# Two Strassen pairs instead of one in three gate/up stages, with the low parts of ten weight chunks made by adding DMA transfers

## The chip, the core and the metric

The kernel runs on one core of a Trainium2 chip: TensorE (PE in the profile) multiplies, VectorE (DVE) and ScalarE (ACT) work on tiles, GpSimd (POOL) does small odd jobs, and SyncE (SP) issues the DMA transfers, which 16 DMA engines carry out. The metric is the device time of one execution in microseconds (us); lower is better.

## The reference

The program is a two-layer transformer trunk on 256 rows of 1024 numbers, in fp32. Each layer is a half-weighted SwiGLU feed-forward block, an attention block, and a second feed-forward block:

```
def rmsnorm(x, g):
    x32 = x.astype(jnp.float32)
    y = x32 * lax.rsqrt(jnp.mean(x32 * x32, axis=-1, keepdims=True) + EPS)
    return (y * g.astype(jnp.float32)).astype(x.dtype)

def swiglu(h, w_gate, w_up, w_down):
    return (jax.nn.silu(h @ w_gate) * (h @ w_up)) @ w_down

    for i in range(DEPTH):
        h = rmsnorm(x, ffn1_norm[i])
        x = x + 0.5 * swiglu(h, ffn1_w_gate[i], ffn1_w_up[i], ffn1_w_down[i])
...
        x = x + jnp.concatenate([o_s, o_m], axis=-1) @ w_out[i]

        h = rmsnorm(x, ffn2_norm[i])
        x = x + 0.5 * swiglu(h, ffn2_w_gate[i], ffn2_w_up[i], ffn2_w_down[i])
```

`w_gate` and `w_up` are 1024 x 2816, `w_down` is 2816 x 1024. There are four feed-forward blocks; the code names them (layer, number): (0, 1), (0, 2), (1, 1), (1, 2). The change touches the gate/up stage (the products with `w_gate` and `w_up`) of the last three.

## The kernel before

**Three products for one.** Every fp32 operand is split in two: a high part `hi`, the value rounded to the type fp32r that TensorE takes, and a low part `lo = value - hi`. A product of two blocks is then three matmuls (`dense`, L498 to L519): hi by hi (L508), lo by hi (L511) and hi by the activations' low part (L514).

**Chunks.** A gate/up stage has 11 groups of 256 columns (`g` = 0 to 10), and each group has two chunks (`c` = 0, 1), halves of the 1024 rows. A chunk, written g/c below, is 512 rows by 256 gate and 256 up columns, 1 MB, laid out as 128 partitions x 2048. It goes through these steps:

- `loader` (L284) issues two 512 KB transfers on SP into a tile `raw`. There are three such tiles (`NRAW`), and a load goes out only when one of them is free.
- `split_hi` (L315) makes `hi` on ScalarE (L335), for a plain chunk in two casts of 128 x 1024. There are four pairs of hi and lo tiles (`NHL`); a chunk's first cast waits until TensorE has used up the chunk four places before it.
- `split_lo` (L339) makes `lo` on VectorE (L353), for a plain chunk in two subtractions of 128 x 1024. When the last is done, the `raw` tile is free.
- TensorE runs 24 matmuls for the chunk: two row blocks of 128, four pieces of 128 rows, three passes (`plain_chunk`, L740).

When both chunks of a group are done, `evac` (L614) applies silu and the product on ScalarE and VectorE, and turns the result by way of DRAM (`hd`, `hr`) for the down products that follow.

**A pair.** `PAIR` (L375) names one pair of groups in each of the last three stages, groups 3 and 4. Its four chunks are taken together as the blocks 11, 12, 22, 21 of a 2 x 2 block product and multiplied by a scheme of Strassen's kind: seven products `m1` to `m7` of 12 matmuls (`product`, L813) instead of eight. Three products use a block as it is (`b11`, `b22`, `b21`), four use a sum of blocks (`t1` to `t4`, `sums` in `pair_items`, L398). A sum takes four VectorE subtractions of 128 x 512 (L347), four casts and four low parts of that size. The seven results are put together by seven VectorE additions (L784). The raw tiles of a pair stay in use long: block 22 is read for `t3` (`m7`), `t2` (`m6`) and `b22` (`m3`), and is free after the low part of `b22`. The order of the chunks and products is a list in `plan_ffn` (L439): seven plain chunks ("p") stand between the products.

**The order of the work.** All engines run their instructions in the order in which the program issues them, each waiting on semaphores. That order is set by a planner in the kernel (`Flow`, from L47): it keeps its own clock with an assumed duration for every step, and issues an instruction when its inputs would be ready by that clock. What the planner assumes decides the order only; on the chip every step takes what it takes.

Of the kernel before, what the change touches and what calls it, by code (L numbers as in the profile page):

```python
# [17 lines left out]
ALU = mybir.AluOpType  # L18
# [124 lines left out]
def kernel(  # L143
# [101 lines left out]
    class Item:  # L245
# [3 lines left out]
        def __init__(self, raws, uses=8, w=1):  # L249
            self.raws, self.uses = raws, uses  # L250
            self.hi = self.lo = None
            self.hit, self.lot, self.st = [None] * 7, [None] * 7, [None] * 4
            self.n, self.frees, self.takes, self.gives, self.guest = 1, 1, 0, 0, False
            self.sums, self.t = [], []
# [26 lines left out]
    def add_chunk(parts, uses=8, w=1):  # L281
        return Item([add_raw(parts)], uses, w)
# [32 lines left out]
    def split_hi():  # L315
        for i, it in enumerate(items):
            yield lambda: (hl_left[0] >= it.n and all(r.raw is not None for r in it.raws)
                           and (xt_room[0] or not it.guest))
            hl_left[0] -= it.n
            if it.guest:  # L320
                xt_room[0] = False
            yield max(r.early or r.arrive for r in it.raws)
            it.hi, it.lo = ([whl.tile([P, 2048], F32R, tag=x, name=f"{x}{i}_{j}") for j in range(it.n)]
                            for x in ("hi", "lo"))
            if it.guest:
                for x, ts in (("xh", it.hi), ("xl", it.lo)):
                    ts += [xtp.tile([P, KT, P], F32R, tag=f"{x}{j}", name=f"g{x}{j}") for j in range(2)]
            for src, q, w, dep in it.units:
                if q == 2:
                    yield max(r.arrive for r in it.raws)  # L330
                if dep is not None:
                    yield lambda: it.st[dep] is not None
                    yield it.st[dep]
                yield calm_a(i)
                nc.scalar.copy(out=it.part(0, q, w), in_=src())  # L335
                t = flow.act(512 * w)
                it.hit[q:q + w] = [t] * w

    def split_lo():  # L339
        for i, it in enumerate(items):  # L340
            if it.sums:
                yield lambda: all(r.raw is not None for r in it.raws) and g2.left >= it.takes + 2
                yield max(r.arrive for r in it.raws)
                it.t += [g2.take([P, 512], F32, "wsum") for _ in range(it.takes)]
                for j, (x, y) in enumerate(it.sums):
                    yield calm_v(i)
                    nc.vector.tensor_sub(it.t[j], x(), y())  # L347
                    it.st[j] = flow.dve(512)
            for src, q, w, dep in it.units:
                yield lambda: it.hit[q] is not None  # L350
                yield it.hit[q]
                yield calm_v(i)
                nc.vector.tensor_sub(it.part(1, q, w), src(), it.part(0, q, w).bitcast(F32))  # L353
# [85 lines left out]
    def plan_ffn(l, nm, wg, wu, wd):  # L439
# [4 lines left out]
            return [q for ab in zip(a, b) for q in ab]  # L444

        gu = {}
        pair = PAIR[l, nm]
        work = [(g, c) for g in range(NG) for c in range(2)]
        if pair is not None:
            rest = [w for w in work if w[0] not in (pair, pair + 1)]  # L450
            n = 2 * pair
            p = iter(rest[n:])
            work = rest[:n]
            loads = {}
# [3 lines left out]
            blocks = {"11": (pair, 0), "12": (pair + 1, 0), "22": (pair + 1, 1), "21": (pair, 1)}  # L458
            raws = [Chunk(parts(*blocks[x])) for x in ("11", "12", "22", "21")]
            made, mk = pair_items(raws)  # L460
            which = dict(zip(("11", "12", "22", "21"), raws))
        for w in work:
            if w in ("11", "12", "22", "21"):
                chunks.append(which[w])
            elif isinstance(w, str):
                mk[w]()
            else:
                gu[w] = add_chunk(parts(*w), 8, 2)
        plan[l, nm, "gu"] = gu
        plan[l, nm, "work"] = [w for w in work if w not in ("11", "12", "22", "21")]  # L470
        if pair is not None:
            plan[l, nm, "pair"] = made
        dn = []
        for c in range(NG):
            dn.append(add_chunk(turned2(wd[l], c)))
# [132 lines left out]
    def ffn(l, nm, xt, gc_next):  # L608
# [142 lines left out]
                if c == 1:  # L751
                    end[tb] = t

        pair = PAIR[l, nm]
        mt, pb = {}, {}
        if pair is not None:
            pit = plan[l, nm, "pair"]
            pps, pend = [[None, None], [None, None]], [[None, None], [None, None]]

        def pair_forms():  # L760

# [17 lines left out]
                g2.give()  # L779
            xt.fm = fm  # L780

        def pair_sums():
            def plus(o, x, m):
                nc.vector.tensor_add(o, x, m)  # L784
                return flow.dve(512)
# [24 lines left out]
                banks.give()  # L810
                pps[g][tb], pend[g][tb] = x, t

        def product(m):  # L813

            name, left = {"m1": ("b11", (0, 0)), "m5": ("t1", 0), "m7": ("t3", 2), "m6": ("t2", 1), "m3": ("b22", 3),
                          "m2": ("b21", (0, 1)), "m4": ("t4", (1, 1))}[m]
            flow.until(banks.has())
            pb[m] = bank("pair_" + m, (P, 512))
            if m == "m1":
                flow.spawn(pair_sums())  # L820
                for e in range(2):
                    flow.spawn(evac(pair + e, pps[e], pend[e], (g2, g2)))
            for k in range(4):
                if isinstance(left, int):
                    flow.until(lambda: xt.ft[left] is not None)
# [5 lines left out]
                t = dense(pb[m], fh, fl, ready, pit[name], k, k == 0, k == 3)  # L831
            mt[m] = t
            if m == "m3":
                g4.give(4)

        if pair is not None:
            flow.spawn(pair_forms())
        work = list(plan[l, nm, "work"])
        if (l, nm) != (0, 1):
# [2 lines left out]
                    plain_chunk(0, c, (tb,))  # L842
            work = work[2:]
        for w in work:
            if isinstance(w, str):
                product(w)
            else:
                plain_chunk(*w, range(2))
        flow.until(banks.has(4))
# [30 lines left out]
            table_hint(AF.Exp)  # L880
        assert xt_room[0]
        xt_room[0] = False
        nxt = None if gc_next is None else Xt(nm == 2 and PAIR[l + 1, 1] is not None)
# [293 lines left out]
    def mixer(l, xt, gc_next):  # L1177
# [386 lines left out]

        flow.until(banks.has(4))
        acc = Acc()
        nxt = Xt(PAIR[l, 2] is not None)
        ids = plan[l, "out"]

        def outp(i, k, tb, hf):  # L1570
# [28 lines left out]
    flow.spawn(split_hi(), idle=True)  # L1599
    flow.spawn(split_lo(), idle=True)  # L1600
    flow.step()
    xt = Xt(PAIR[0, 1] is not None)

    def start_gain():
        tp = bank("gps0")
# [88 lines left out]
```

## Time and profile before

| | |
|---|---|
| median of three runs | 957.13 us (956.89 to 957.25) |
| the profiled execution | 956.95 us |
| its span in the trace | 955.2 us |
| granted TensorE clock | 1.0 throughout |
| TensorE, VectorE, ScalarE, GpSimd busy | 99%, 83%, 61%, 12% of the span |
| bytes moved by DMA | 204.03 MB, 214 GB/s on average |

The gate/up stage of block (0, 2) begins at 317.5 us in the trace and is the one followed in the prediction. In the profile, a row of a timeline has the start in us, the duration in us, the engine, the line of the code, the operation, and what it writes and reads; in brackets stand the idle time just before it and what ended that. A row of groups ends with the busy time, the mean duration in ns, and the idle time before. `raw`, `hi`, `lo`, `wsum` (a sum of blocks), `gu` (a plain group's result in PSUM), `pair_m` (a Strassen product's result), `xh` and `xl` (the parts of the activations) are tiles of the program.

### The profile page before, as it was taken

Reading aid. Unit: us, or ns where it says so; the run is one execution under the profiler, and the core shown is the slowest. Engines: PE = TensorE matmul, PEld = TensorE weight load, DVE = VectorE, ACT = ScalarE, POOL = GpSimd, SP = SyncE. Lnnn points to the kernel's source line nnn. Section 1 sums busy time; section 2 is a strip of 40 time slices with the busy share of each in tenths; the row PEclk is TensorE's granted clock in tenths of the full one; section 3 lists DMA queues with packets and bytes.
Section 4 is the critical chain, followed back from the end, with each engine's and each line's share of the span. In section 5 each row is a group of like instructions: output and inputs, shape, how many; then the busy total and the mean of one; then the engine's idle time right before and its main releaser. Section 6 shows DMA issues by size and latency. Waiting matters only on the chain.

```text
span 955.2 us, 13249 instructions
## 1 busy us (share of the span) xinstructions
PE 946.8 (99%) x4489; PEld 777.3 (81%) x4489; DVE 796.1 (83%) x1437; ACT 578.6 (61%) x1102; POOL 110.7 (12%) x160
## 2 busy tenths in 40 slices
PE   8999999999999999999999999999999999999998
PEld 7888888888877888888888888888887778888886
DVE  6767767688787899989889899896999888998884
ACT  6655555677676756647646656563676865665650
POOL 1000088322110100000000000000434200000000
PEclk9999999999999999999999999999999999999999
DMA  9988878486525376787746769775641367589751
GB/s 287 326 260 284 260 249 262 154 272 212 177 90 163 102 248 226 242 301 232 240 144 219 231 204 298 247 254 170 208 152 56 122 212 228 180 267 286 238 196 44
DMA packets 169294, 204.03 MB, mean 214 GB/s; under 512 B 9673, under 2 KB 144394, under 8 KB 169226
## 3 DMA queue, kind: packets, MB, share of 16 engines
q1 hardware_dynamic: 169226, 203.18, 66.3%
q8 instruction: 35, 0.57, 0.3%
q14 instruction: 33, 0.27, 0.1%
HBM read 188.99 MB, written 14.16 MB: 213 GB/s over the span
## 4 chain that ended last, share of the span: by engine, by line
PE 93%; DVE 4%; ACT 1%; DMA 1%; issue 0%; SPq 0%
PE gu L514 14%; PE gu L508 14%; PE gu L511 14%; PE acc L508 9%; PE acc L514 9%; PE acc L511 9%; PE pj L514 3%; PE pj L511 3%; PE pj L508 3%; PE pair_m L514 2%; PE pair_m L511 2%; PE pair_m L508 2%; DVE lo L353 1%; PE S L1335 1%; PE xtp L522 1%; PE AV L1416 1%
## 5 line engine op out<-in xcount | busy, mean ns | idle before, releaser
L335 ACT CAST hi<-raw 128x512 fp32r<-128x512 f32 (+1 forms) x469 | 339.1, 771 | 194.3 <-PE gu L514 75.5
L353 DVE TENSOR_TENSOR lo<-raw,hi 128x512 fp32r<-128x512 f32 (+1 forms) x469 | 394.6, 877 | 67.7 <-ACT hi L335 66.7
L514 PE MATMUL gu<-hi,xl 128*128 128x512 f32 x608 | 236.9, 390 | 0.4 <-DVE xl L559 0.4
L511 PE MATMUL gu<-lo,xh 128*128 128x512 f32 x608 | 236.8, 389 | 0.0
L508 PE MATMUL gu<-hi,xh 128*128 128x512 f32 x608 | 236.8, 389 | 0.0
L514 PEld LDWEIGHTS gu<-hi,xl 128*128 128x128 f32 x608 | 114.1, 188 | 24.5 <-DVE xl L559 0.8
L508 PEld LDWEIGHTS gu<-hi,xh 128*128 128x128 f32 x608 | 114.2, 188 | 23.5
L511 PEld LDWEIGHTS gu<-lo,xh 128*128 128x128 f32 x608 | 114.1, 188 | 23.5
L514 PE MATMUL acc<-hi,ht 128*128 128x512 f32 x280 | 109.5, 391 | 0.0
L508 PE MATMUL acc<-hi,ht 128*128 128x512 f32 x280 | 109.3, 390 | 0.0
L511 PE MATMUL acc<-lo,ht 128*128 128x512 f32 x280 | 109.1, 390 | 0.0
L511 PE MATMUL pj<-lo,xh 128*128 128x512 f32 x160 | 63.9, 400 | 0.0
L514 PE MATMUL pj<-hi,xl 128*128 128x512 f32 x160 | 63.8, 399 | 0.0
L508 PE MATMUL pj<-hi,xh 128*128 128x512 f32 x160 | 63.8, 399 | 0.0
L529 POOL TENSOR_TENSOR xr<-v,nhalf 128x1 f32<-128x1 f32 x12 | 11.7, 974 | 445.0 <-DVE v L527 445.0
L511 PEld LDWEIGHTS acc<-lo,ht 128*128 128x128 f32 x280 | 52.6, 188 | 10.9
L514 PEld LDWEIGHTS acc<-hi,ht 128*128 128x128 f32 x280 | 52.6, 188 | 10.8
L508 PEld LDWEIGHTS acc<-hi,ht 128*128 128x128 f32 x280 | 52.6, 188 | 10.7
L335 ACT CAST hi<-wsum 128x512 fp32r<-128x512 f32 x66 | 38.9, 620 | 20.5 <-DVE wsum L347 20.4
L623 ACT ACTIVATE sil<-gu,xr 128x256 f32<-128x256 f32 x76 | 35.7, 470 | 25.0 <-PE gu L514 24.9
L353 DVE TENSOR_TENSOR lo<-wsum,hi 128x512 fp32r<-128x512 f32 x66 | 42.5, 678 | 0.0
L529 POOL TENSOR_TENSOR hf<-v,nhalf 128x8 f32<-128x8 f32 (+1 forms) x20 | 31.7, 1584 | 90.1 <-DVE v L527 81.8
(231 smaller groups left out, 1356.6 us busy)
## 6 DMA issues: line engine op xcount, KB each, us to landing
raw<-in_ffn_w_down_dram SPq DMA_DIRECT2D x176, 256.0 KB, 4.3
raw<-in_ffn_w_gate_dram SPq DMA_DIRECT2D x86, 512.0 KB, 4.2
raw<-in_ffn_w_up_dram SPq DMA_DIRECT2D x86, 512.0 KB, 5.4
raw<-in_w_in_dram SPq DMA_DIRECT2D x32, 512.0 KB, 5.4
hd<-hb SPq DMA_DIRECT2D x44, 256.0 KB, 4.5
hr<-hd SPq DMA_DIRECT2D x44, 256.0 KB, 4.4
raw<-in_w_out_dram SPq DMA_DIRECT2D x8, 1024.0 KB, 4.8
raw<-in_w_mem_kv_dram SPq DMA_DIRECT2D x4, 1024.0 KB, 5.5
```

Source lines behind the costliest of these rows:

```text
L335: nc.scalar.copy(out=it.part(0, q, w), in_=src())
L353: nc.vector.tensor_sub(it.part(1, q, w), src(), it.part(0, q, w).bitcast(F32))
L508: nc.tensor.matmul(out=ps, lhsT=xh, rhs=wh, start=start, stop=False)
L511: nc.tensor.matmul(out=ps, lhsT=xh, rhs=wl, start=False, stop=False)
L514: nc.tensor.matmul(out=ps, lhsT=xl, rhs=wh, start=False, stop=stop)
L522: nc.tensor.transpose(out=dst, in_=src, identity=flip if flipped else ident)
L529: nc.gpsimd.tensor_tensor(out=dst, in0=v[:, :n], in1=nhalf[:, :n], op=ALU.pow)
L623: nc.scalar.activation(sil, ps[tb][:, 0:256], AF.Silu, scale=xt.r[tb])
L1335: nc.tensor.matmul(out=ss[e][:, pr, :nk], lhsT=q[rows, pr, :], rhs=k[rows, pr, :], start=i == 0, stop=i == len(passes) - 1)
L1416: nc.tensor.matmul(out=av[64 * e:64 * e + 64, pr, :], lhsT=vsrc(kb, pr, e), rhs=pts[e][:, pr, kb, :], start=(kb == 0), stop=(kb == nb - 1))
```

## The change

Each of the last three gate/up stages now has two pairs, groups 2 and 3, and 4 and 5. With fewer plain chunks left, four instead of seven plain chunks stand between the products of a pair. Ten plain chunks of each of these stages (1/0, 1/1, and all of groups 6 to 9) get their low part in another way: ScalarE writes `hi` and then `-hi` into the lo tile (four passes of 128 x 1024 in place of two), and GpSimd issues one transfer of 1 MB from `raw` to `lo` that adds to what is there (`accum_op=ALU.add`). VectorE does nothing for these chunks. The raw tile is free when the transfer has landed. Chunks 0/0, 0/1, 10/0 and 10/1 stay as they were.

```
+            if it.by_dma:
+                flow.spawn(lo_by_dma(it))
...
+                if it.by_dma:
+                    nc.scalar.activation(it.part(1, q, w), src(), AF.Copy, scale=-1.0)
+                    t = flow.act(512 * w)
...
+    def lo_by_dma(it):
+
+        t = it.hit[3]
+        yield t
+        nc.gpsimd.dma_start(out=it.lo[0], in_=it.raws[0].raw, accum_op=ALU.add)
+        t = flow.now + 7.0
+        it.lot[0:4] = [t] * 4
+        yield t
+        raw_left[0] += it.frees
...
-    PAIR = {(0, 1): None, (0, 2): 3, (1, 1): 3, (1, 2): 3}
+    TEN = ((1, 0), (1, 1), (6, 0), (6, 1), (7, 0), (7, 1), (8, 0), (8, 1), (9, 0), (9, 1))
+    BY_DMA = {(0, 1): (), (0, 2): TEN, (1, 1): TEN, (1, 2): TEN}
+    PAIR = {(0, 1): (), (0, 2): (2, 4), (1, 1): (2, 4), (1, 2): (2, 4)}
...
-            for x in ("11", "m1", "p", "12", "m5", "p", "22", "m7", "p", "m6", "p", "m3", "p", "p", "21", "m2", "p", "m4"):
-                work.append(next(p) if x == "p" else x)
...
+            order = (("11", "m1", "p", "12", "m5", "p", "22", "m7", "p", "m6", "p", "m3", "p", "p", "21", "m2", "p", "m4")
+                     if len(pairs) == 1 else
+                     ("11", "m1", "p", "12", "m5", "22", "m7", "p", "m6", "p", "m3", "21", "m2", "p", "m4"))
```

The rest of the diff passes the number of the pair through `product` and `pair_sums`, so that two pairs can be open in one stage. So TensorE's order in such a stage is now: 0/0, 0/1, 1/0, 1/1, then m1, 6/0, m5, m7, 6/1, m6, 7/0, m3, m2, 7/1, m4 for the first pair, the same with 8/0, 8/1, 9/0, 9/1 for the second, then 10/0, 10/1. Its list has 36 matmuls fewer than before (3972 rows of instructions instead of 4008).

On SP, in the first pair of block (0, 2), the loads stood like this before (raw55 to raw59 are the fifth to the ninth chunk of the stage, `hd` and `hr` the way of a finished group through DRAM; the brackets name the semaphores waited for, DVE for VectorE, DMAHW for transfers that SP issued):

```order
L291 DMA raw56_3340<-in_ffn2_w_gate_dram 128x4x256 [waits DMAHW5_49,DMAHW4_49,DVE_49]
L291 DMA raw56_3340<-in_ffn2_w_up_dram 128x4x256
L291 DMA raw57_3369<-in_ffn2_w_gate_dram 128x4x256 [waits DMAHW7_49,DMAHW6_49,DVE_49]
L291 DMA raw57_3369<-in_ffn2_w_up_dram 128x4x256
L291 DMA raw58_3445<-in_ffn2_w_gate_dram 128x4x256 [waits DMAHW0_49,DMAHW1_49,DVE_49,Activation_49]
L291 DMA raw58_3445<-in_ffn2_w_up_dram 128x4x256
L640 DMA hd_3461<-hb_3383 128x512 [waits DVE_49]
L291 DMA raw59_3478<-in_ffn2_w_gate_dram 128x4x256 [waits DMAHW2_49,DMAHW3_49,DVE_49,Activation_49]
L291 DMA raw59_3478<-in_ffn2_w_up_dram 128x4x256
```

And now (raw56 is chunk 6/0, raw57 block 12, raw58 block 22, raw59 chunk 6/1; DMASW is a transfer that GpSimd issued, numbered 0 for chunk 1/0, 1 for 1/1, 2 for 6/0):

```order
L292 DMA raw56_3413<-in_ffn2_w_gate_dram 128x4x256 [waits DMAHW4_49,DMAHW5_49,DMASW0_49,Activation_49]
L292 DMA raw56_3413<-in_ffn2_w_up_dram 128x4x256
L659 DMA hd_3455<-hb_3366 128x512 [waits DVE_49]
L292 DMA raw57_3460<-in_ffn2_w_gate_dram 128x4x256 [waits DMAHW6_49,DMAHW7_49,DMASW1_49,Activation_49]
L292 DMA raw57_3460<-in_ffn2_w_up_dram 128x4x256
L665 DMA hr_3492<-hd_3455 128x4x128 [waits DMAHW4_49,PE_49]
L659 DMA hd_3536<-hb_3489 128x512 [waits DMAHW0_49,DVE_49]
L292 DMA raw58_3540<-in_ffn2_w_gate_dram 128x4x256 [waits DMAHW2_49,DMAHW1_49,DMAHW3_49,DMASW2_49,Activation_49]
L292 DMA raw58_3540<-in_ffn2_w_up_dram 128x4x256
L292 DMA raw59_3543<-in_ffn2_w_gate_dram 128x4x256
L292 DMA raw59_3543<-in_ffn2_w_up_dram 128x4x256
```

The loads of 6/0, block 12 and block 22 wait for adding transfers in place of VectorE, and the load of 6/1 stands right behind that of block 22.

On ScalarE, before, around the first two products of the pair (hi60 is a plain chunk, hi61 is `t1`):

```order
L335 CAST hi60_0_3605<-raw60_3531 128x1024
L623 ACTIVATE sil_3611<-gu1_3511,xr_2978 128x256
L335 CAST hi60_0_3605<-raw60_3531 128x1024
L791 COPY gu_u_3635<-pair_m1_3608 128x512
L335 CAST hi61_0_3640<-wsum_3642 128x512
L335 CAST hi61_0_3640<-wsum_3643 128x512
L335 CAST hi61_0_3640<-wsum_3644 128x512
L335 CAST hi61_0_3640<-wsum_3645 128x512
```

And now, from `t3` (hi58) over chunk 6/1 (hi59, lo59) to `t2` (hi60):

```order
L336 CAST hi58_0_3568<-wsum_3570 128x512
L336 CAST hi58_0_3568<-wsum_3571 128x512
L336 CAST hi58_0_3568<-wsum_3572 128x512
L336 CAST hi58_0_3568<-wsum_3573 128x512
L336 CAST hi59_0_3599<-raw59_3543 128x1024
L339 ACTIVATE lo59_0_3600<-raw59_3543 128x1024
L336 CAST hi59_0_3599<-raw59_3543 128x1024
L339 ACTIVATE lo59_0_3600<-raw59_3543 128x1024
L336 CAST hi60_0_3623<-wsum_3496 128x512
```

A chunk of the new kind has four passes in a row on ScalarE, and those of 6/1 come behind the four casts of `t3`, which is made from block 22.

More of the change, by code (lines that the diff above doesn't have):

```diff
@@ L446, in plan_ffn @@
         gu = {}
-        pair = PAIR[l, nm]
         work = [(g, c) for g in range(NG) for c in range(2)]
[L449 to L454, printed above, removed]
-            for x in ("11", "m1", "p", "12", "m5", "p", "22", "m7", "p", "m6", "p", "m3", "p", "p", "21", "m2", "p", "m4"):
-                work.append(next(p) if x == "p" else x)
+        pairs, sets, blocks = PAIR[l, nm], {}, {}
@@ L457, in plan_ffn @@
             work += list(p)
[L458 to L461, printed above, removed]
         for w in work:
[L463 to L466, printed above, removed]
+            if w in blocks:
+                chunks.append(blocks[w])
+            elif isinstance(w[0], str):
+                sets[w[1]][1][w[0]]()
@@ L752, in plain_chunk @@
                     end[tb] = t
[L754 to L758, printed above, removed]
+        pairs, pit = PAIR[l, nm], plan[l, nm, "pair"]
+        mts, pbs = ({a: {} for a in pairs} for _ in range(2))
         def pair_forms():
@@ L1601 @@
     flow.step()
-    xt = Xt(PAIR[0, 1] is not None)
+    xt = Xt(bool(PAIR[0, 1]))
     def start_gain():
```

41 lines of the change are left out of this document (27 added, 14 removed).

## The prediction

> **What bounds the kernel now.** I read the page's first part, then the groups by line and shape, then who waited for whom on SP, then timelines of one gate/up stage, that of block (0, 2). The page says that TensorE is hardly ever idle:
>
> ```profile
> PE 946.8 (99%) x4489; PEld 777.3 (81%) x4489; DVE 796.1 (83%) x1437; ACT 578.6 (61%) x1102; POOL 110.7 (12%) x160
> ```
>
> So the time falls only by giving TensorE less, as long as every other engine keeps up. The table by stretches shows how near they are in the stage (columns: span; busy us of PE, PEld, DVE, ACT, POOL; granted clock; share of the DMA engines; GB/s). The second row is a stretch with the DMA engines full:
>
> ```profile
> 322.00:440.00 118.00, 118.00 (x524) 97.77 (x523) 106.62 (x170) 69.85 (x109) 0.94 (x1) 1.00 0.75 241
> 425.00:430.00 5.00, 5.00 (x24) 4.14 (x23) 4.20 (x9) 1.00 (x2) 0.00 (x0) 1.00 1.01 360
> ```
>
> VectorE is at 90%, ScalarE at 59%, the DMA engines at 75%. Full DMA engines move 360 GB/s, so 1 MB takes 1.05 / 0.36 = 2.9 us on the wire. What keeps DMA from its limit is in SP's waits:
>
> ```profile
> SPq L291 <- DVE lo L353: 433.7, 114, 21.9
> ```
>
> A load of weights stands 433.7 us in all waiting for a low part, that is, for one of the three raw tiles. The weights come late because tiles are few, and this costs nothing now since low parts are early. How early, the stage's beginning shows. On SP and VectorE:
>
> ```profile
> 306.77 0.37 SPq L291 DMA_DIRECT2D raw<-in_ffn_w_gate_dram  x1
> 321.45 0.37 SPq L291 DMA_DIRECT2D raw<-in_ffn_w_gate_dram  x1
> 321.86 0.51 SPq L291 DMA_DIRECT2D raw<-in_ffn_w_up_dram  x1
> ...
> 320.20 1.22 DVE L353 TENSOR_TENSOR lo<-raw,hi 128x1024 fp32r<-128x1024 f32 x1
> 325.55 0.68 DVE L559 TENSOR_TENSOR xl<-y,xh 128x512 fp32r<-128x512 f32 x1
> ```
>
> The low part of chunk 1/0 ends at 320.20 + 1.22 = 321.42, and at 321.45 the load that needed its tile goes out. On ScalarE:
>
> ```profile
> 315.88 1.05 ACT L335 CAST hi<-raw 128x1024 fp32r<-128x1024 f32 x1
> 316.95 1.28 ACT L895 ACT_TABLE_LOAD   x1
> 318.35 0.61 ACT L557 CAST xh<-y 128x512 fp32r<-128x512 f32 x1
> 318.86 1.05 ACT L335 CAST hi<-raw 128x1024 fp32r<-128x1024 f32 x1
> ...
> 323.40 0.62 ACT L557 CAST xh<-y 128x512 fp32r<-128x512 f32 x1 [0.98 <-DVE y L554]
> 323.93 0.47 ACT L623 ACTIVATE sil<-gu,xr 128x256 f32<-128x256 f32 x1
> ...
> 326.33 2.01 ACT L335 CAST hi<-raw 128x1024 fp32r<-128x1024 f32 x2 [1.32 <-PE gu L514]
> 329.05 1.06 ACT L335 CAST hi<-raw 128x1024 fp32r<-128x1024 f32 x1 [0.20 <-PE gu L514]
> 334.49 2.01 ACT L335 CAST hi<-raw 128x1024 fp32r<-128x1024 f32 x2 [1.52 <-PE gu L514]
> 339.97 1.05 ACT L335 CAST hi<-raw 128x1024 fp32r<-128x1024 f32 x1 [2.29 <-PE gu L514]
> ```
>
> The waits for PE at 329.05, 334.49 and 339.97 mark the ends of chunks 0/1, 1/0 and 1/1: 5.46 us per chunk. So the low part of 1/0, ready at 321.42, is 7.6 us ahead of its turn. Two casts in a row take 2.01 us: 0.96 from one to the next, and four take 3.9 with the wake-up.
>
> **What the change takes from TensorE.** Three more pairs, each with one product of 12 matmuls less. Their pace is in TensorE's timeline, 16 matmuls between these two rows:
>
> ```profile
> 324.32 0.39 PE L511 MATMUL gu<-lo,xh 128*128 128x512 f32 x1
> ...
> 327.94 0.39 PE L514 MATMUL gu<-hi,xl 128*128 128x512 f32 x1
> ```
>
> (327.94 - 324.32) / 16 = 0.226 us, so 36 matmuls are 8.1 us. A product is 2.7 us.
>
> **VectorE and ScalarE.**
>
> ```profile
> L353 DVE TENSOR_TENSOR lo<-raw,hi 128x1024 fp32r<-128x1024 f32 x166 | 198.5, 1216 | 34.3 <-ACT hi L335 33.5 <-DMA grow<-in_mem_q_norm_dram 0.7
> L335 ACT CAST hi<-raw 128x1024 fp32r<-128x1024 f32 x166 | 168.8, 1049 | 106.0 <-PE gu L514 58.2 <-DMA raw<-in_ffn_w_up_dram 28.2 <-issue 10.6
> L353 DVE TENSOR_TENSOR lo<-wsum,hi 128x512 fp32r<-128x512 f32 x66 | 42.5, 678 | 0.0
> L335 ACT CAST hi<-wsum 128x512 fp32r<-128x512 f32 x66 | 38.9, 620 | 20.5 <-DVE wsum L347 20.4
> L347 DVE TENSOR_TENSOR wsum<-raw,wsum 128x512 f32<-128x512 f32 x42 | 27.8, 679 | 0.2
> L784 DVE TENSOR_TENSOR gu_v<-gu_v,pair_m 128x512 f32<-128x512 f32 x15 | 10.0, 683 | 0.2
> ```
>
> Per stage VectorE loses ten low parts (20 x 1.216 = 24.3 us) and gains, for the second pair, 16 sums and 16 low parts of 128 x 512 (32 x 0.68 = 21.8), one plain low part less (-2.4) and 7 additions (4.8): 24.2 us. It comes out even. ScalarE gains 20 passes (21.0 us) and, for the pair, 16 casts less two wide ones (9.9 - 2.1) and a copy: about 29 us, so 99 of some 115. Neither total is the bound; the order in which things become ready is.
>
> **The adding transfer, X.** Let X be the time from the last ScalarE pass of a chunk to the landing of its low part. No transfer in the trace adds, and none is issued by GpSimd. The nearest rows are that of 1 MB loads on the page (the last number is the median time from issue to landing in us),
>
> ```profile
> raw<-in_w_out_dram SPq DMA_DIRECT2D x8, 1024.0 KB, 4.8
> ```
>
> and those of the two halves of a chunk in this stage:
>
> ```profile
> raw<-in_ffn_w_gate_dram SPq DMA_DIRECT2D x15, 512.0 KB, 4.4
> raw<-in_ffn_w_up_dram SPq DMA_DIRECT2D x15, 512.0 KB, 5.4
> ```
>
> If the addition is free on the way, X = 4.8. If the second operand costs the wire as much as the first, X = 4.8 + 2.9 = 7.7. Two operands have to be fetched, so I take X = 7.0, nearer to the upper end. By the Trainium skill (Collectives: The Full Stack, "The bandwidth ceiling: the fold count and why AG ≠ RS ≠ AR"), an adding transfer issues two reads for each piece written and ran at about half a copy's rate (32.35 against 62.28 GB/s); no run here shows it, and by it X would be the 7.7 and the total below 1029 us. A load, from the issue of its first half to the landing of its second, takes 0.4 + 5.4 = 5.8 us; a load issued right behind it lands 2.9 later.
>
> VectorE does two sums in a row in 1.25 us, 0.6 from one to the next:
>
> ```profile
> 344.09 1.25 DVE L347 TENSOR_TENSOR wsum<-raw,raw 128x512 f32<-128x512 f32 x2
> ```
>
> **The chain of raw tiles, in block (0, 2).** In place of a low part on VectorE (about 1.2 us behind its cast), a tile is now held for two more passes and X. Step by step:
>
> 1. Chunk 1/0: on ScalarE the wide pass at 315.88 gets a second behind it, then the table load, an `xh`, two more passes: end at about 321.8, landing at 321.8 + X. The passes of 1/1 (two ahead of the second `xh`) push that `xh` from 323.40 to about 325.8, and `xl` from 326.2 to 327.0: TensorE, which needs it at 326.2, waits 0.8.
> 2. The load of 6/0 waits for that landing (DMASW0). It lands 5.8 later, four passes take 3.9, and X again: low part at 331.5 + 2X. Its turn on TensorE is at 340.0 + 0.8 + 2.7 (m1) = 343.5. Wait: 2X - 12.0.
> 3. The load of block 22 waits for the landing of 6/0 (DMASW2); call that moment a. Queued behind it on SP is the load of 6/1. Block 22 lands at a + 5.8; after four sums, a cast and a low part of `t3` m7 can begin, at a + 9.0, against a + 5.46 + 2.7 for 6/0 and m5: wait 0.8. Chunk 6/1 lands at a + 8.7, its passes come behind the casts of `t3`, and its low part is there at a + 12.7 + X. Its turn is at a + 11.7. Wait: X + 1.0.
> 4. Chunk 7/1: block 22's tile is free after the low part of `b22`, whose casts stand behind the passes of 7/0; from a this is 10.8 (low parts of `t3`), 5.8 (load), 3.9 (passes), 3.5 (`b22`), then 5.8 + 3.9 + X for 7/1 itself: a + 33.7 + X. TensorE, from the landing of 6/1, has 19.1 us before it: a + 31.8 + X. Wait 1.9. Chunk 9/1 in the second pair: the same, 1.9.
> 5. Chunk 8/0: its load waits for the low parts of `t4`, whose four casts stand behind the passes of 7/1 (end p) and take, with the last low part, 3.2: p + 3.2 + 5.8 + 3.9 + X, against p + X + 5.46 + 2.7 + 2.7. Wait 2.0.
> 6. Chunk 8/1: its load waits for the landing of 8/0 (DMASW6) and shares the wire with block 22's: 6.6 + 3.9 + X, against 10.9. Wait X - 0.4.
>
> The sum is 0.8 + (2X - 12.0) + 0.8 + (X + 1.0) + 2 x 1.9 + 2.0 + (X - 0.4) = 4X - 4.0 per stage: 24.0 us for X = 7.0. On GpSimd the second `xr` stands behind the transfers of 1/0 and 1/1; it would run at about 328.3, ahead of the `sil` that needs it after 329: nothing. Three stages of like order: 72.0 us. Against the profiled execution's 956.95 us (span 955.2; the median of the runs is 957.13): 956.95 - 8.1 + 72.0 = 1020.8, **1021 us**.
>
> For X = 4.8, chunk 6/0 is 2.4 us early and its wait and m7's go; 6/1 waits 4.2, 8/1 4.4; with the 6.6 of the small ones 15.2 per stage: 994 us. If the small waits are covered too, by loads that land faster than the median, 8.6 per stage: 975 us. For X = 10, 36 per stage: 1057 us.
>
> **The rivals.** *It gets faster.* If the low part lands within 3.4 us, chunk 6/0 is early by 12.0 - 2X and the wait of 6/1 (X + 1.0 less that, without m7's) is gone; with quicker loads the small waits go as well, and the 8.1 us are won: 949 us. Against it speaks that even a plain 1 MB takes 4.8. For it, that this row is a median under load and that steps 3 to 6 add medians. 0.09. A tie, waits of about 8 us in all: 0.05. An outcome within 0.2%, 2 us, is about what a measurement here can't tell from none.
>
> *The DMA engines become the bound.* The stage uses 0.75 x 118 = 88 us of them; ten adding transfers are 29 us at one operand and 58 at two. That makes 117 to 146 of a stage of about 139 with the waits. At the upper end the loads and X lengthen together; with X of 10 to 12 the waits are 36 to 44 per stage, and the time is 1057 to 1081. For it: stretches at 1.01 exist already. Against it: the engines pause whenever tiles are held. 0.14. By the Trainium skill (DMA: Bandwidth & Descriptors, "Issuing engines are not separate DMA queues") transfers issued by GpSimd run on the same engines as SP's; no GpSimd transfer is in this trace.
>
> *The change not doing what it says* is excluded by the list of TensorE's instructions: 36 matmuls are gone.
>
> **How the numbers follow.** The chain of tiles 0.72, DMA as the bound 0.14, faster 0.09, a tie 0.05. The range reaches from 975 (X = 4.8 and no small waits) to 1070, halfway into the DMA case; outside lie faster and tie (0.14) and the rest of DMA (0.05). Slower has 0.86.
>
> **What would show it.** Right: on TensorE, waits for the transfers `lo<-raw`, longest at 6/1 and 8/1 in each stage, about 8 and 7 us; on SP, loads waiting for them; the first adding transfer landing about 7 us behind its last pass; a gate/up stage 21 us longer than before. Wrong: landings under 3.4 us, or TensorE idle for less than 10 us more than now.

## The result, and the profile after

The changed kernel takes 1100.26 us (median of 4 runs, 1097.3 to 1101.55); the kernel before, on the same chip, 957.12 (956.89 to 957.25). The ratio is 1.148 (95% interval 1.146 to 1.151): slower, as forecast, but by 143 us where 64 were forecast, and outside the range. The profiled execution took 1101.55 us, its span is 1099.8.

The page's first part, and the row of GpSimd's queue (packets, MB, share of 16 engines' span):

```profile
PE 981.1 (89%) x4453; PEld 793.1 (72%) x4453; DVE 794.7 (72%) x1488; ACT 659.1 (60%) x1207; POOL 135.2 (12%) x190
...
q0 software_dynamic: 4320, 31.46, 15.2%
```

TensorE has 36 matmuls fewer, VectorE came out even (796.1 before) and ScalarE got 80.5 us more, 27 per stage: these steps were right. But TensorE now idles 1099.8 - 981.1 = 118.7 us of the span (8.4 before), and is busy 34 us longer in spite of the fewer matmuls. Who waited for whom, first on TensorE, then on SP (us in total, times, longest):

```profile
PE gu L530 <- DMA lo<-raw: 92.9, 22, 9.0
PE gu L530 <- ACT hi L336: 16.6, 2, 9.1
```

```profile
SPq L292 <- DVE lo L371: 307.3, 80, 21.9
SPq L292 <- DMA lo<-raw: 174.9, 27, 21.7
```

TensorE waits for the adding transfers, and SP's loads wait for them too. Inside the stage of block (0, 2) these are TensorE's waits, in order of time: chunks 1/1, 6/0, 6/1, 7/1, 8/0, 8/1, 9/1 (start, us, and in brackets the idle time before and its releaser):

```profile
336.61 0.50 PE L530 MATMUL gu<-lo,xh 128*128 128x512 f32 x1 [1.38 <-DMA lo<-raw]
...
351.95 0.77 PE L530 MATMUL gu<-lo,xh 128*128 128x512 f32 x1 [6.88 <-DMA lo<-raw]
...
373.22 0.77 PE L530 MATMUL gu<-lo,xh 128*128 128x512 f32 x1 [8.39 <-DMA lo<-raw]
...
400.49 0.77 PE L530 MATMUL gu<-lo,xh 128*128 128x512 f32 x1 [5.63 <-DMA lo<-raw]
...
415.68 0.47 PE L530 MATMUL gu<-lo,xh 128*128 128x512 f32 x1 [2.66 <-DMA lo<-raw]
...
435.94 0.77 PE L530 MATMUL gu<-lo,xh 128*128 128x512 f32 x1 [7.50 <-ACT hi L336]
...
462.12 0.77 PE L530 MATMUL gu<-lo,xh 128*128 128x512 f32 x1 [4.50 <-DMA lo<-raw]
```

The wait of 8/1 is put down to ScalarE, but SP's next load, which waits for the landing of 8/1, goes out at 435.86, in the same moment, so this wait too is for the adding transfer. The places are those of the prediction's steps (only the 1.38 at 1/1 was not forecast), and 6/1 and 8/1 are the longest; 6/0 (forecast 2.0), 7/1 and 9/1 (1.9 each) are far longer than forecast. The length of the stage can be read from the rows of `sil`, one for each finished group (before, then after; the two times are the first and last start):

```profile
L623 ACT ACTIVATE sil<-gu,xr x18: 457/468/476, 323.9 to 436.9; 128x256 f32<-128x256 f32 x18
```

```profile
L642 ACT ACTIVATE sil<-gu,xr x14: 452/471/476, 323.2 to 485.2; 128x256 f32<-128x256 f32 x14
```

113.0 us became 162.0. All three stages grew alike, by 45 to 49 us, 142 us together; the rest of the kernel kept its length within 3 us. Adding the 2.7 us that the product less saves, the new delay is 50 us per stage, where the sum had 24.0. The transfers of the stage (KB each, median us from issue to landing, from 317 to 440 us):

```profile
lo<-raw POOLq DMA_DIRECT2D x9, 1024.0 KB, 7.5
raw<-in_ffn_w_gate_dram SPq DMA_DIRECT2D x15, 512.0 KB, 5.7
raw<-in_ffn_w_up_dram SPq DMA_DIRECT2D x15, 512.0 KB, 9.3
```

The adding transfer is near its forecast: X was 7.3 to 8.8 us in nine of the ten chunks, and 10.8 in chunk 7/0. But the second half of a load lands in 9.3 us, where 5.4 was used. The rows show which loads: SP's issue of the first halves of 6/0, 7/1, 8/0 and 9/1 (the rows at 373.15 and 435.86 are the loads of block 21 in the two pairs), ScalarE's first pass over each of the four chunks, and GpSimd's adding transfers of 1/1, 7/0, 7/1 and 9/0:

```profile
329.51 0.37 SPq L292 DMA_DIRECT2D raw<-in_ffn_w_gate_dram  x1
...
373.15 0.37 SPq L292 DMA_DIRECT2D raw<-in_ffn_w_gate_dram  x1
...
376.10 0.38 SPq L292 DMA_DIRECT2D raw<-in_ffn_w_gate_dram  x1
...
394.12 0.37 SPq L292 DMA_DIRECT2D raw<-in_ffn_w_gate_dram  x1
...
435.86 0.37 SPq L292 DMA_DIRECT2D raw<-in_ffn_w_gate_dram  x1
...
438.31 0.37 SPq L292 DMA_DIRECT2D raw<-in_ffn_w_gate_dram  x1
```

```profile
340.63 1.05 ACT L336 CAST hi<-raw 128x1024 fp32r<-128x1024 f32 x1 [7.11 <-DMA raw<-in_ffn_w_up_dram]
...
387.85 1.06 ACT L336 CAST hi<-raw 128x1024 fp32r<-128x1024 f32 x1 [0.65 <-DMA raw<-in_ffn_w_up_dram]
...
403.51 1.05 ACT L336 CAST hi<-raw 128x1024 fp32r<-128x1024 f32 x1 [3.73 <-DMA raw<-in_ffn_w_up_dram]
...
449.49 1.05 ACT L336 CAST hi<-raw 128x1024 fp32r<-128x1024 f32 x1 [0.65 <-DMA raw<-in_ffn_w_up_dram]
```

```profile
328.33 0.87 POOL L349 DMA_DIRECT2D lo<-raw  x1 [5.07 <-ACT lo L339]
...
373.04 0.85 POOL L349 DMA_DIRECT2D lo<-raw  x1 [6.03 <-ACT lo L339]
392.05 0.85 POOL L349 DMA_DIRECT2D lo<-raw  x1 [18.16 <-PE pair_m L533]
...
435.25 0.86 POOL L349 DMA_DIRECT2D lo<-raw  x1 [5.52 <-ACT lo L339]
```

These loads took 11.1, 11.8, 9.4 and 11.2 us, and each went out 1.2 to 3.1 us behind an adding transfer of another chunk. Those of 7/1 and 9/1 also had the load of block 21 in front, 3.0 and 2.5 us ahead. A second thing that the prediction had left out stands in TensorE's granted clock (last but two of each row; first number after the span is PE's busy time):

```profile
340.00:345.00 5.00, 5.00 (x23) 3.86 (x21) 0.08 (x1) 4.26 (x5) 0.17 (x1) 1.00 0.71 221
345.00:350.00 5.00, 0.07 (x1) 0.00 (x0) 5.00 (x11) 3.75 (x7) 0.72 (x1) 0.88 0.77 157
350.00:355.00 5.00, 3.05 (x7) 2.48 (x8) 1.86 (x4) 0.00 (x0) 0.00 (x0) 0.50 0.77 218
355.00:360.00 5.00, 5.00 (x22) 4.06 (x21) 2.75 (x5) 1.96 (x4) 0.00 (x0) 0.93 1.06 342
```

TensorE stops at 345.07. The mean of 0.88 over the second stretch means 1.2 us at half clock, so the clock fell at about 348.8, 3.7 us after the stop. TensorE goes on at 351.95; the 0.93 of the last stretch means another 0.7 us at half, so the clock was back at about 355.7, after 3.7 us of work. By the Trainium skill (TensorE: Matmul & The Clock Gate, "Part 1: The HAM clock gate") the array drops to half clock after an idle window of about 3.4 us and returns after about 3.4 us of steady work; the trace agrees for this wait, and the run with the pairs alone, below, shows that the clock also falls beside shorter ones. TensorE is busy 34 us longer with 8.1 us less to do, so its matmuls became 42 us longer over the kernel.

### The profile page after: what moved, and what is told of

Its sections match the earlier page's. It is cut to its first block, busy times and chain, and to the rows that moved or that the text cites. A ratio compares the mean times of both kernels' runs of the same rounds, so it can differ in the third digit from the quotient of the medians.

```text
span 1099.8 us, 13460 instructions
## 1 busy us (share of the span) xinstructions
PE 981.1 (89%) x4453; PEld 793.1 (72%) x4453; DVE 794.7 (72%) x1488; ACT 659.1 (60%) x1207; POOL 135.2 (12%) x190
## 3 DMA queue, kind: packets, MB, share of 16 engines
q0 software_dynamic: 4320, 31.46, 15.2%
## 4 chain that ended last, share of the span: by engine, by line
PE 54%; DMA 22%; DVE 8%; ACT 8%; issue 6%; SPq 1%; POOL 0%; ACTq 0%; POOLq 0%; DVEq 0%
DMA raw<-in_ffn_w_up_dram 12%; DMA lo<-raw 9%; PE acc L527 7%; PE acc L530 7%; PE acc L533 7%; PE gu L530 6%; PE gu L533 6%; PE gu L527 6%; ACT hi L336 5%; DVE lo L371 3%; ACT lo L339 3%; PE pj L533 2%; PE pj L527 2%; PE pj L530 2%; SPq L292 1%
## 5 line engine op out<-in xcount | busy, mean ns | idle before, releaser
L371 DVE TENSOR_TENSOR lo<-raw,hi 128x512 fp32r<-128x512 f32 (+1 forms) x403 | 317.1, 822 | 122.9 <-ACT hi L336 122.6
L530 PE MATMUL gu<-lo,xh 128*128 128x512 f32 x512 | 216.7, 423 | 109.5 <-DMA lo<-raw 92.9
L533 PE MATMUL gu<-hi,xl 128*128 128x512 f32 x512 | 212.9, 416 | 0.0
L527 PE MATMUL gu<-hi,xh 128*128 128x512 f32 x512 | 211.7, 413 | 0.2 <-ACT xh L576 0.2
L527 PEld LDWEIGHTS gu<-hi,xh 128*128 128x128 f32 x512 | 104.0, 203 | 24.0 <-ACT xh L576 0.9
L336 ACT CAST hi<-wsum 128x512 fp32r<-128x512 f32 x114 | 66.7, 619 | 65.2 <-DVE wsum L365 59.2
L371 DVE TENSOR_TENSOR lo<-wsum,hi 128x512 fp32r<-128x512 f32 x114 | 73.2, 680 | 4.8 <-ACT hi L336 4.8
L645 DVE SCALAR_TENSOR_TENSOR h<-gu,xr,sil 128x256 f32<-128x256 f32 x64 | 30.6, 479 | 60.1 <-ACT sil L642 59.8
L349 POOL DMA_DIRECT2D lo<-raw x30 | 26.2, 872 | 371.6 <-ACT lo L339 255.5
L339 ACT ACTIVATE lo<-raw 128x1024 fp32r<-128x1024 f32 x60 | 63.3, 1055 | 0.0
```

Source lines behind the costliest of these rows:

```text
L339: nc.scalar.activation(it.part(1, q, w), src(), AF.Copy, scale=-1.0)
L349: nc.gpsimd.dma_start(out=it.lo[0], in_=it.raws[0].raw, accum_op=ALU.add)
L527: nc.tensor.matmul(out=ps, lhsT=xh, rhs=wh, start=start, stop=False)
L530: nc.tensor.matmul(out=ps, lhsT=xh, rhs=wl, start=False, stop=False)
L533: nc.tensor.matmul(out=ps, lhsT=xl, rhs=wh, start=False, stop=stop)
L645: nc.vector.scalar_tensor_tensor(out=h, in0=ps[tb][:, 256:512], scalar=xt.r[tb], in1=sil, op0=ALU.mult, op1=ALU.mult)
```

## The experiments

Theory A throughout is the prediction's: tiles are held longer, and the chain load, passes, adding transfer, next load decides. The rivals change from one set of runs to the next, and so do the letters C and D: each expectation says what it sets against A. One execution of each kernel was timed; the kernel before took 957.3 to 959.0 us beside them.

**The pairs alone, and the adding transfers alone.**

```
-    BY_DMA = {(0, 1): (), (0, 2): TEN, (1, 1): TEN, (1, 2): TEN}
+    BY_DMA = {(0, 1): (), (0, 2): (), (1, 1): (), (1, 2): ()}
```

> Two pairs in each of the three stages, all low parts on VectorE again. Theory A (the waits come from raw tiles that are held over four passes and an adding transfer): no waits for transfers are left and the clock stays at 1.0; VectorE has some 24 us more per stage than before, about 131 of 115, and becomes the bound, 10 to 16 us of waits per stage for low parts: 980 to 1000 us. Theory B (the two pairs with only four plain chunks between their products hold the raw tiles too long by themselves): waits of 30 us and more per stage stay, 1060 to 1100 us.

```
-    PAIR = {(0, 1): (), (0, 2): (2, 4), (1, 1): (2, 4), (1, 2): (2, 4)}
+    PAIR = {(0, 1): (), (0, 2): (3,), (1, 1): (3,), (1, 2): (3,)}
```

> One pair per stage as before the change, but the ten chunks (groups 1 and 6 to 9) get their low parts by adding transfers. Theory A: the waits stay, somewhat fewer since more plain chunks lie between the products, 20 to 35 us per stage with slow clock behind them: 1030 to 1090 us. Theory B: the waits go with the second pair, 950 to 965 us.

The pairs alone take 990.35 us, the transfers alone (with one pair) 1049.91. Of the first, the page's busy times and TensorE's waits:

```profile
PE 954.9 (97%) x4453; PEld 774.6 (78%) x4453; DVE 858.2 (87%) x1548; ACT 603.0 (61%) x1147; POOL 109.5 (11%) x160
```

```profile
PE gu L530 <- DVE lo L371: 11.3, 11, 2.4
PE pair_m L530 <- DVE lo L371: 10.3, 6, 2.4
```

Without adding transfers VectorE is late by 1 or 2 us at a time, and no wait reaches 3 us. The clock did not stay at 1.0 as expected: its mean is 0.989, from six stretches of 3.4 us at half. One of them follows a stretch in which TensorE was busy for 1.56 of 3.40 us (columns: span, PE's busy time, granted clock, share of the DMA engines, GB/s):

```profile
394.20:397.60 3.40, 1.56 (x6) 1.00 0.99 331
397.60:401.00 3.40, 3.09 (x7) 0.50 0.77 232
```

The transfers without the second pair already cost 93 us. So both parts cost by themselves, the transfers more, and the sum of the two (33 + 93) is near the whole (143).

**A plain copy in place of the adding one**, so that the addition is left out and the low parts hold a copy of raw:

```
-        nc.gpsimd.dma_start(out=it.lo[0], in_=it.raws[0].raw, accum_op=ALU.add)
+        nc.gpsimd.dma_start(out=it.lo[0], in_=it.raws[0].raw)
```

> The change with the transfer from raw to lo copying in place of adding (the low part is then the whole value, so the addition is left out). If the second operand is what makes the landing late: landing 2.9 us earlier (median 5.3 in place of 8.2), waits 10 us less per stage: 1050 to 1070 us. If the time goes to GpSimd's issue and to sharing the DMA engines with the loads: landing 7.5 us or more, 1090 to 1102 us.

1024.22 us. The rows of the queue and of the transfers:

```profile
q0 software_dynamic: 4320, 31.46, 8.5%
...
lo<-raw POOLq DMA_DIRECT2D x30, 1024.0 KB, 5.4
```

The landing came as expected, 2.8 us earlier, but the time fell by 76 us, more than the 30 to 50 expected. The row of q0 says why there was more to win: the same 31.46 MB occupied the 16 engines for 8.5% of 1022.5 us = 87 us each, with the addition for 15.2% of 1099.8 = 167 us, 1.9 times as long. By the Trainium skill (Collectives: The Full Stack, "The bandwidth ceiling: the fold count and why AG ≠ RS ≠ AR") an add in a transfer needs two source reads, told there of a reduce-scatter between cores; the 1.9 agrees. And the loads of 6/0, 7/1 and 9/1 took 7.5, 6.4 and 6.1 us here, from the rows of SP and ScalarE, where with the addition they took over 11. (The load of block 21 also stood further ahead of the last two here, 5.7 and 5.2 us.)

**The clock kept up** by small products into a spare bank ahead of six chunks of each stage, where TensorE waits:

```
+    DUMMY = {(6, 0): 30, (6, 1): 36, (7, 1): 22, (8, 0): 10, (8, 1): 32, (9, 1): 18}
...
+            for _ in range(n):
+                nc.tensor.matmul(out=d[:, 0, :], lhsT=ident, rhs=ident, start=True, stop=True)
```

> The change with small matmuls (128 x 128, 0.21 us each, 10 to 36 of them, results thrown away) ahead of the six chunks of a stage whose waits were longest, so that TensorE does not stand idle there. If the slow clock behind the waits is a cost of its own: clock 1.0, and 30 to 42 us less, 1058 to 1070 us. If the chain of tiles sets the time and a slower TensorE only shortens the next wait: clock 1.0, and less than 15 us gained, 1085 to 1100 us.

1095.94 us, mean granted clock 0.992 in place of 0.947 (the small products took 0.11 us each and not 0.21). GpSimd's last adding transfer of the stage shows what that was worth (this run; in the changed kernel it went out at 453.70):

```profile
454.35 0.86 POOL L349 DMA_DIRECT2D lo<-raw  x1 [17.78 <-ACT lo L339]
```

All ten transfers go out within 0.7 us of where they did at half clock. The slow matmuls only fill time in which TensorE would have waited for the next tile: of 42 us some 4 come back. The slow clock is a symptom here, and hardly a term of the sum.

**Four raw tiles** (four of the small tiles for sums are given up for the fourth):

```
-    NRAW, NHL, NT2 = 3, 4, 19
+    NRAW, NHL, NT2 = 4, 4, 15
```

> The change with four raw tiles in place of three (room for it from four of the 19 small work tiles). Theory A (raw tiles held over the passes and the adding transfer release the loads late): a load no longer waits for the landing just before it; what is left is the chunk's own four passes, load and landing behind the release of its hi tile, 4 + 8.5 against 10.9 us, every second time: waits of about 10 us per stage, 975 to 1010 us. Theory C (the DMA engines carry three operands per added chunk and are the bound): the loads start earlier but land later, 1060 to 1095 us.

1046.41 us, between what the two theories said. A fourth tile wins 54 us, so tiles are part of it; but the loads that now go out earlier meet the adding transfers all the same, in the stage (317 to 440 us):

```profile
raw<-in_ffn_w_gate_dram SPq DMA_DIRECT2D x16, 512.0 KB, 7.9
raw<-in_ffn_w_up_dram SPq DMA_DIRECT2D x16, 512.0 KB, 8.5
```

**The raw tile let go ahead of the adding transfer**, which reads the weights once more from DRAM:

```
-        nc.gpsimd.dma_start(out=it.lo[0], in_=it.raws[0].raw, accum_op=ALU.add)
+        for dst, src in it.raws[0].parts:
+            nc.gpsimd.dma_start(out=dst(it.lo[0]), in_=src, accum_op=ALU.add)
```

> The change with the adding transfers reading the weights from DRAM a second time in place of the raw tile, so that the raw tile is free after the four passes. Theory A: the loads no longer wait for landings; the waits fall to a half or less, 990 to 1040 us, although HBM gives 30 MB more. Theory C (the DMA engines are the bound): no better, 1080 to 1130 us, since the wire carries as much.

1120.6 us. The tile is free as soon as the passes end, and the kernel is slower still:

```profile
PE gu L530 <- DMA lo<-in_ffn_w_up_dram: 131.2, 18, 13.1
```

The two adding transfers per chunk land 9.7 and 13.3 us behind their issue (page's medians), and TensorE waits for them directly. Theory A's number for this run fell, and that of theory C (1080 to 1130) held. But the transfer itself changed as well: the page counts 31680 packets for it in place of 4320, and 17.6% of 1118.8 = 197 us on each engine in place of 167. So the run shows that a tile let go early does not help when the low part lands later; what a held tile costs by itself it does not show.

**The adding transfer in two halves**, each behind its own two passes:

```
-        nc.gpsimd.dma_start(out=it.lo[0], in_=it.raws[0].raw, accum_op=ALU.add)
+        nc.gpsimd.dma_start(out=it.part(1, q, w), in_=src(), accum_op=ALU.add)
```

> The change with the adding transfer cut in two, the first half issued behind the first two passes. Theory A: the first half's landing comes 1.9 us earlier and the second half, with half the bytes, about 2 us earlier; X falls by about 2 us and with it the waits by 8 to 18 us per stage: 1045 to 1075 us. Theory C: the same bytes on the wire, 1090 to 1105 us.

1079.22 us, 21 less, and 4 us outside theory A's range. The page's median from issue to landing, 5.8 us, is that of all halves; the second halves, which let the tile go, landed 7.2 us behind their issue (median of the trace's landings), 1.0 less than the whole transfer's 8.2. The bytes kept the engines as long as before (16.3% of 1077.4 = 176 us). The plain copy, with a landing of 5.4 and half the time on the wire, won much more.

**Load on the engines without the late landing, and the late landing without the load.** In both the addition is left out. The first sends a second transfer behind each copy, for which nothing of the chain waits:

```
+        d = dram.tile([P, 2048], F32, tag="spare", name="spare", bufs=2)
+        nc.gpsimd.dma_start(out=d, in_=it.hi[0].bitcast(F32))
```

> As in the run with a plain copy, the adding transfer is a plain transfer of raw into lo (the addition is left out, so the low parts are wrong), and behind each one GpSimd issues a second 1 MB transfer, of hi into a spare piece of DRAM, for which no product and no raw tile waits. So the low part lands as early as a plain copy lets it, but the DMA engines carry about as much as with the adding transfers. Theory A (both terms count: the landing itself comes 2.8 us later with the addition, which by the sum 4X - 4 is 11.2 us per stage, 34 us in all, and the rest of the 76 us between copy and addition is loads that land later beside the fuller engines): 1050 to 1085 us. Rival C (only the landing of the low part counts): 1024 to 1040. Rival D (only the load on the engines counts): 1085 to 1110.

The second lets GpSimd work ahead of the copy:

```
+        for j in range(10):
...
+            nc.gpsimd.tensor_tensor(out=idle, in0=a, in1=b, op=ALU.mult)
```

> Plain transfer of raw into lo (the addition is left out), and ahead of each one GpSimd does ten small multiplications, about 3 us in all, that wait for the last ScalarE pass. So the low part lands about as late behind the last pass as with the addition, while the DMA engines carry only the plain copy. Theory A: 1045 to 1070 us (11.2 us per stage more than the 1024 us of the plain copy). Rival C (only the landing counts): 1085 to 1110. Rival D (only the load on the engines): 1024 to 1035.

The first takes 1072.83 us, the second 1114.61. The first had the same occupancy as the additions,

```profile
q0 software_dynamic: 8640, 62.92, 15.2%
...
lo<-raw POOLq DMA_DIRECT2D x30, 1024.0 KB, 5.8
```

and the landing 0.4 us later than with the copy alone (1.2 in the stage of block (0, 2), 6.7 for 5.5, which by 4X - 4 is 5 us per stage at most), and lost 49 us of the 76. Its loads of 6/0, 7/1 and 9/1 took 7.9, 9.6 and 10.0 us, where the copy alone had 7.5, 6.4 and 6.1, with block 21's load as far ahead as there (5.7 and 5.2 us); ScalarE's first pass over 7/1 stands 9.6 behind SP's issue at 375.50:

```profile
385.06 1.05 ACT L336 CAST hi<-raw 128x1024 fp32r<-128x1024 f32 x1 [4.75 <-DMA raw<-in_ffn_w_up_dram]
```

So loads that land late because the engines carry more cost time by themselves; the rivals that let only one of the two count both fall. The second run lies above all three ranges. It overshot its purpose: in this stage the ten multiplications took 3.1 to 5.9 us, not 3, the most at 7/1,

```profile
388.15 0.41 POOL L352 TENSOR_TENSOR idle<-lo 128x32 f32<-128x32 f32 x1 [13.38 <-ACT lo L340]
388.65 5.37 POOL L352 TENSOR_TENSOR idle<-idle 128x32 f32<-128x32 f32 x9
394.25 0.59 POOL L353 DMA_DIRECT2D lo<-raw  x1 [0.24 <-issue]
```

so that X was 8.5, 8.0, 10.5 and 9.6 us for the four chunks of the 4X (1/0, 6/0, 6/1, 8/1), which gives 36.6 - 4 = 33 us per stage. The loads of 7/1 and 9/1 took 10.6 and 10.5 us in spite of the plain copies, with block 21's load only 1.0 us in front of them: 9.5 more. X was 12.0 for 8/0 and 11.4 for 9/1, later than for the chunks ahead of them: some 3 more. And on ScalarE a `sil` stands between the second and the third pass of 8/0 and waited for TensorE, which was itself waiting at 7/1:

```profile
403.71 0.47 ACT L646 ACTIVATE sil<-gu,xr 128x256 f32<-128x256 f32 x1 [6.71 <-PE gu L537]
```

With these 7 the sum is 53 of about 54 us. The run shows that a late landing is dear by itself: it lost 90 us against the plain copy, with no more on the wire (7.4% of 1112.8 = 82 us).

**Fewer adding transfers.** Six, four, and then the seven that leave out 1/1, 7/0 and 9/0:

```
+    TEN = ((1, 0), (1, 1), (7, 0), (7, 1), (9, 0), (9, 1))
```

> Chunks 6/0, 6/1, 8/0 and 8/1 go back to low parts on VectorE; 1/0, 1/1, 7/0, 7/1, 9/0 and 9/1 keep adding transfers. Theory A (what costs time is tiles held by the chunks whose tile the next urgent block or chunk waits for; those four are the chunks in which the long waits begin): most of the waits go, 970 to 1005 us, with VectorE near 97% in these stages. Rival D (each adding transfer costs its share of the engines, so six of ten cost about six tenths of the 110 us between the pairs alone and the whole change): 1045 to 1065.

```
+    TEN = ((1, 0), (1, 1), (7, 0), (9, 0))
```

> Only 1/0, 1/1, 7/0 and 9/0 keep adding transfers, the other six go back to VectorE. Theory A: 965 to 990 us, below the 990 us of the pairs without any adding transfer, because VectorE loses 9.7 us per stage and no long chain begins at these four. Rival D: 1030 to 1040.

```
+    TEN = ((1, 0), (6, 0), (6, 1), (7, 1), (8, 0), (8, 1), (9, 1))
```

> Chunks 1/1, 7/0 and 9/0 go back to low parts on VectorE, the other seven keep adding transfers. These three are those whose adding transfer is on the way when the loads of 6/0, 7/1 and 9/1 go out; in the changed kernel those three loads take 11.1, 11.7 and 11.1 us from the issue of the first half to the first ScalarE pass. Theory A in its present form (a load issued beside an adding transfer lands about 5 us late, three times per stage, and the chain of tiles hands that on): the three loads take 7 us or less, and the time falls by 3 x 16 us and a little to 1035 to 1060 us. Rival C (a chunk costs what TensorE waits for its own low part; for these three together at most 2.5 us per stage): 1085 to 1100. Rival D (each adding transfer costs an equal share of the 110 us): 1060 to 1075.

1048.1, 1046.51 and 1054.88 us. The first two are misses for theory A as it then stood. Rival D's number held for six (1045 to 1065) and not for four (1030 to 1040); that six and four take the same time speaks against it. With four, TensorE's two long waits of the stage are at 7/0 and 9/0:

```profile
375.74 0.76 PE L530 MATMUL gu<-lo,xh 128*128 128x512 f32 x1 [9.08 <-DMA lo<-raw]
...
432.71 0.77 PE L530 MATMUL gu<-lo,xh 128*128 128x512 f32 x1 [7.27 <-DMA lo<-raw]
```

These two hardly waited in the changed kernel (0.65 at 7/0), since TensorE was already late from 6/1 and 8/1. Taking a chunk's transfer away moves the wait to the next chunk that has one; four transfers keep half of the 110 us that all ten add to the pairs alone (1046.51 against 990.35 and 1100.26).

The last of the three was chosen by the loads: it takes away the transfers beside which the loads of 6/0, 7/1 and 9/1 had gone out, though TensorE had waited only 2 us per stage for those three chunks. It gave 45 us, inside the 1035 to 1060 of theory A. SP's issue of 6/0, and ScalarE's first pass over it:

```profile
330.25 0.37 SPq L292 DMA_DIRECT2D raw<-in_ffn_w_gate_dram  x1
```

```profile
335.66 1.05 ACT L336 CAST hi<-raw 128x1024 fp32r<-128x1024 f32 x1 [3.22 <-DMA raw<-in_ffn_w_up_dram]
```

5.4 us in place of 11.1. For 7/1 and 9/1 the passes began when TensorE freed a tile, but the trace has the landings: 8.4 and 7.7 us behind SP's issue, with no adding transfer on the way and block 21's load 1.1 and 1.0 us in front. So the "7 us or less" held for 6/0 alone, and the load of block 21 is a part of the late loads of 7/1 and 9/1. The run also takes away what these chunks held of the tiles, so the 45 us are not the loads' alone.

## Why the prediction was wrong

**Right, with its mechanism.** The 36 matmuls, VectorE's even sum (1.4 us off over the kernel), ScalarE's 27 us per stage (29 forecast), GpSimd's second `xr` without cost to TensorE, and the chain of raw tiles as what decides, with its waits in the order and at the places given. The first landing came 7.7 us behind its last pass (7.0). The 0.8 of step 1 was 0.6.

**The step that failed: the load in steps 2 to 6.** "It lands 5.8 later" was taken from medians of the kernel before, where no adding transfer ran. In each stage four loads on the chain go out right behind an adding transfer, which keeps the engines about twice as long as a copy. Those of 6/0, 7/1 and 9/1 took 11.1, 11.8 and 11.2 us, 5.3 + 6.0 + 5.4 = 16.7 more than the sum's. That of 8/0 took 9.4, 3.6 more, of which some 2.3 are left in step 5, since the low parts of `t4` were ready earlier and X was less than for 7/1. The two loads behind one another in step 3 took 10.1 from SP's issue to the first pass of 6/1 instead of 8.7, and that of 8/1 8.8 instead of 6.6: 3.6 more, with no adding transfer on the way. That is 23 us per stage. By the Trainium skill (DMA: Bandwidth & Descriptors, "Queues, rings and completion order") each engine takes turns, packet by packet, between the queues that it has work for. A load beside another transfer would then run slower; the rows agree, and the price is theirs.

Not all of it is the adding transfer's. Step 4 also left out block 21's load, which goes out 3.0 and 2.5 us ahead of those of 7/1 and 9/1. By the 2.9 us that 1 MB takes on the wire, up to 2.9 us of the 6.0 and of the 5.4 are its share, an estimate; the runs in which it stands 1.0 to 1.1 us ahead of the load of 7/1 (10.6 us beside a plain copy; 8.4 to the landing with no adding transfer on the way) show that it counts, and do not part the two exactly.

**X, a smaller miss.** 7.7 for 1/0, and 7.3 for 6/0, 6/1 and 8/1, instead of 7.0 add 1.6, and the longer 8.7 of 7/1 and 9/1 against the 7.3 of the chunks ahead of them 2.8: 4 us per stage.

With both, the sum is 24 + 23 + 4 = 51 us for the stage followed, which grew by 49.0 + 2.7 = 52, and 957 - 8.1 + 3 x 51 = 1102 for 1101.55. It is put together after the fact from this one stage, so its agreement says less than a forecast's would; in the other two stages the same loads go out behind adding transfers, that of 6/0 with a landing after about 9 us instead of 11, and they grew by 45 and 48 + 2.7. The run with a second transfer behind a plain copy lost 16 us per stage, at most 5 of them by X, so load on the engines is worth some 11 by itself. The runs with four and six transfers show that the sum can't be cut up by chunks: it holds for the whole chain only.

**The rival with the DMA engines as the bound** (0.14, 1057 to 1081) came nearer to the cause. It said that the loads and X lengthen together, with X of 10 to 12; the loads grew, and X stayed at 7.3 to 8.8 in nine of ten chunks. The engines are at 86% in the stage (322 to 484 us), though full in stretches (1.06 in the last row of the clock table). What cost was that loads on the chain and adding transfers fall on the same microseconds: the load of 6/0 goes out on the landing of 1/0, 1.2 us behind the transfer of 1/1, and those of 7/1 and 9/1 wait for the low part of `b22`, whose casts stand on ScalarE right behind the passes of 7/0 and 9/0. It deserved more than 0.14.

**The slow clock** was not in the sum and hardly needed a term: 42 us of longer matmuls, and about 4 us back when it was kept up. What stays open is how the 23 us divide between adding transfers and the other loads. No version came below the kernel before: without any adding transfer VectorE is late and the kernel takes 33 us more, and each set of adding transfers tried costs more than that.

## What to carry to other kernels

When a change hands work to DMA, price the other transfers again at the moments at which it will run, not only the new one: where the same engine's passes start a transfer and let a load go, the two meet every time, and a median from a trace without the new traffic is the wrong row. Sum up a chain of buffers with every link at its price under sharing, and treat a chunk's own wait as where the delay shows, not as what that chunk costs. A slower engine downstream of the chain (here TensorE at half clock) costs almost nothing while it only fills the wait for the next buffer.

## What the runs showed of the hardware

- An adding transfer of 1 MB within SBUF occupied the DMA engines 1.9 times as long as a plain copy (167 against 87 us for 31.46 MB) and landed in 8.2 us instead of 5.4. GpSimd took 0.87 us to issue it, 0.53 for the copy:

```profile
L349 POOL DMA_DIRECT2D lo<-raw x30: 527/528/805, 321.9 to 936.0; - x30
```

- In the stage followed, a 1 MB load issued 1 to 3 us behind such a transfer took 9.4 to 11.8 us until it could be used, two of the four with another load in front; with no such transfer on the way, 5.4 (chunk 6/0 in the last run), and 7.7 and 8.4 us to the landing with another load 1 us in front.
- In the changed kernel TensorE's clock stood at 0.50 in 16 stretches of 3.4 to 10.2 us, each at a wait of 2.7 us or more: 42 us of longer matmuls, nearly all of it hidden. With the pairs alone it did so for 3.4 us six times, though no wait was longer than 2.5 us.
- Ten multiplications of 128x32 in a row on GpSimd took 3.1 to 5.9 us.
